# Products of a tile of weights in two groups: first with its high part, then with its low part

## The chip, the cores and the metric

The kernel runs on one core of a Trainium2 chip. The metric is device time in microseconds of one execution, the median of three runs. TensorE multiplies, VectorE, ScalarE and GpSimd work on tiles in on-chip memory, and SyncE issues the transfers from DRAM.

## The reference

Two layers of a decoder trunk on 256 tokens of 1024 features. Each layer is a feed-forward half-step, token mixing (a gated delta rule beside sparse attention, one input and one output projection), and a second feed-forward half-step; the scale, shift and gate of each come from a conditioning vector. One norm ends it. All weights are float32 and are read from DRAM once (256 MB).

```python
for l in range(DEPTH):
    mod = (cond @ ada_w[l] + ada_b[l]).reshape(B, 3, 3, D)
    h = modulate(rms_norm(x, norm_g[l, 0]), mod[:, 0, 0], mod[:, 0, 1])
    x = x + 0.5 * mod[:, 0, 2][:, None, :] * swiglu(h, ffn_w_in[l, 0], ffn_w_out[l, 0])
    h = modulate(rms_norm(x, norm_g[l, 1]), mod[:, 1, 0], mod[:, 1, 1])
    x = x + mod[:, 1, 2][:, None, :] * token_mix(h, mix_w_in[l], ..., mix_w_out[l], cos, sin)
    h = modulate(rms_norm(x, norm_g[l, 2]), mod[:, 2, 0], mod[:, 2, 1])
    x = x + 0.5 * mod[:, 2, 2][:, None, :] * swiglu(h, ffn_w_in[l, 1], ffn_w_out[l, 1])
return rms_norm(x, final_norm_g)
```

## The kernel before, in words

Products run in float32r, a shortened float32. For accuracy each operand is split in two such parts, a high one and a low one that holds what the high one lost, and a product becomes three: high with high, high with low, low with high.

**The stream of weights.** Weights come as 344 tiles of 128 partitions by up to 1024 columns (`raw`, 10 slots). `produce` (line 726) lets ScalarE make the high part (`hi`, 4 slots) and VectorE the low one (`lo<-raw,hi`, 4 slots), which waits for the high part. A tile serves 24 products on 128 x 256 columns as a rule (8 pairs of a weight block and a feature block, three products each). Between the tiles stand 36 pieces of the conditioning (`ada`): each reads 2 MB and is multiplied and summed by VectorE, and in part by ScalarE (`adb`, `raw<-raw,cond`) and GpSimd (`adb<-adb,raw`). `take` (line 753) hands the next tile to the products.

**The products.** `split_mm` (line 1018) issues three of one weight block: `hi` with the high part of the features (`hh`, `aa` or `yh`), `hi` with their low part (`hl`, the second half of `aa`, `yl`), and `lo` with the high part. `split_mm_nat` (line 1211) does it with tokens as weights, in the projections `n0` to `n2`. `early_mm` (line 1011) does it on x before its norm is known, scaled by feature: `xh` from ScalarE and `xl` from VectorE, made block by block of 128 features in `norm_xa` as the sublayer before finishes a block of x (`xT`). So a sublayer begins while the last norm is being summed (`nS`, `nsq`, `nv`, `nr`).

The feed-forward step (`ffn_body`, line 1060) has 11 units of four tiles each into two banks (gate and value side by side), then 4 units of six tiles out of the hidden features (`aa`), two banks each. `ffn_act` makes the hidden features: `sg` and `aa` on ScalarE, `av` and the low `aa` on VectorE. Token mixing (`mix_body`, line 1174) projects, runs the delta rule and the attention as streams beside each other, and `mix_out` (line 1855) projects back.

**What sets the order.** Nothing is issued where it is written. `record` (line 276) notes every instruction and what it depends on; products of one bank keep their recorded order. `schedule` (line 362) then walks a list scheduler over the whole program with estimated times, forward and backward in turn, and keeps the order whose estimated end is first. `issue` puts out that order, so every instruction has line 546 in the profile, and tiles must be told apart by name. Each engine runs its own instructions strictly in that order.

## Time and profile before

| | us |
|---|---|
| median of three runs (1206.88, 1209.07, 1210.11) | 1209.07 |
| span of the profiled execution | 1203.7 |
| TensorE busy with products | 1160.3 |
| TensorE busy with weight loads | 1080.6 |
| VectorE busy | 958.1 |
| ScalarE busy | 669.8 |
| GpSimd busy | 219.6 |

The span is of one profiled execution, from its first instruction to its last. Products and weight loads of TensorE overlap; the ends of products are modelled, so a busy TensorE may still have short gaps between the starts of products. In the names, buffer numbers are left out: `bank<-hh,lo` is a product of the features `hh` with a low part of weights into a bank.

### The profile page before, as it was taken

What the parts mean: (1) busy time and instruction counts of PE and PEld (TensorE: products, weight loads), DVE (VectorE), ACT (ScalarE), POOL (GpSimd) and SP (SyncE); (2) the same over time, 40 slices, a digit from 0 to 9 for tenths busy, and PEclk for the clock granted to TensorE, in tenths of its full rate; (3) what the DMA queues carried; (4) which work ended last, traced back from release to release, by engine and by line L of the source; (5) the groups of instructions that cost most, each with busy time, mean ns of one, the idle gap of its engine ahead of it and who ended that gap; (6) DMA issues with size and microseconds to landing.
All of it is one profiled execution on the core that took longest, in us unless ns stands there. A gap on an engine that the chain in (4) does not pass through costs nothing.

```text
span 1203.7 us, 24132 instructions
## 1 busy us (share of the span) xinstructions
PE 1160.3 (96%) x9450; PEld 1080.6 (90%) x9451; DVE 958.1 (80%) x1716; ACT 669.8 (56%) x1177; POOL 219.6 (18%) x184
## 2 busy tenths in 40 slices
PE   8998989999999999999999999999999999999997
PEld 3698989997988899999999999998797879999997
DVE  3699899898987699988978877999998669855543
ACT  2456446555585556556545454556657556644444
POOL 2033343220001233113221110233100013200001
PEclk9999999999999999999999999999999999999999
DMA  9879999985424378987976887988562235756540
GB/s 333 292 218 313 293 303 308 287 254 171 132 54 123 118 225 294 301 272 227 319 224 187 284 265 221 314 283 283 157 192 55 71 102 181 255 172 193 181 145 36
DMA packets 230758, 259.89 MB, mean 216 GB/s; under 512 B 16130, under 2 KB 190836, under 8 KB 230644
## 3 DMA queue, kind: packets, MB, share of 16 engines
q1 hardware_dynamic: 230644, 258.35, 68.0%
q8 instruction: 74, 1.21, 0.4%
q14 instruction: 40, 0.33, 0.1%
HBM read 256.09 MB, written 2.23 MB: 215 GB/s over the span
## 4 chain that ended last, share of the span: by engine, by line
PE 72%; DVE 16%; DMA 4%; issue 3%; ACT 3%; POOL 1%; DVEq 0%; POOLq 0%; ACTq 0%; SPq 0%
PE bank L546 72%; DVE lo L546 7%; DVE ada L546 2%; ACT hi L546 2%; DMA raw<-in_ffn_w_out_dram 1%; DMA raw<-in_ada_w_dram 1%; DVE qT L546 1%; DVE aa L546 1%; POOL adb L546 1%; DMA raw<-in_ffn_w_in_dram 1%; DMA w<-in_cmp_w_k_dram 1%; DVE av L546 0%; DVE hl L546 0%; DVE KL L546 0%; DVE Pt L546 0%
## 5 line engine op out<-in xcount | busy, mean ns | idle before, releaser
L546 DVE TENSOR_TENSOR lo<-raw,hi 128x1024 fp32r<-128x1024 f32 (+3 forms) x340 | 420.2, 1254 | 119.6 <-ACT hi L546 86.4
L546 ACT ACTIVATE hi<-raw 128x1024 fp32r<-128x1024 f32 (+3 forms) x340 | 344.6, 1028 | 282.1 <-PE bank L546 233.2
L546 PE MATMUL bank<-hh,lo 128*128 128x256 f32 x1440 | 380.2, 285 | 10.4 <-DVE lo L546 10.3
L546 PE MATMUL bank<-hl,hi 128*128 128x256 f32 x1440 | 385.0, 284 | 0.6 <-DVE hl L546 0.6
L546 PE MATMUL bank<-hh,hi 128*128 128x256 f32 x1440 | 384.0, 283 | 1.6 <-ACT hi L546 1.0
L546 PEld LDWEIGHTS bank<-hh,lo 128*128 128x128 f32 x1440 | 260.2, 189 | 14.4 <-DVE lo L546 13.9
L546 PEld LDWEIGHTS bank<-hh,hi 128*128 128x128 f32 x1440 | 264.1, 189 | 4.7 <-issue 1.7
L546 PEld LDWEIGHTS bank<-hl,hi 128*128 128x128 f32 x1440 | 264.2, 189 | 1.2 <-DVE hl L546 0.8
L546 PE MATMUL bank<-aa,hi 128*128 128x256 f32 x1408 | 247.7, 281 | 2.9 <-ACT hi L546 2.5
L546 PEld LDWEIGHTS bank<-aa,hi 128*128 128x128 f32 x1408 | 212.5, 189 | 3.4 <-ACT hi L546 2.7
L546 PE MATMUL bank<-aa,lo 128*128 128x256 f32 x704 | 188.4, 283 | 8.5 <-DVE lo L546 8.5
L546 POOL TENSOR_TENSOR adb<-adb,raw 128x512 f32<-128x512 f32 x65 | 98.4, 1514 | 305.2 <-ACT raw L546 283.9
L546 PEld LDWEIGHTS bank<-aa,lo 128*128 128x128 f32 x704 | 129.5, 189 | 11.2 <-DVE lo L546 11.1
L546 DVE SCALAR_TENSOR_TENSOR ada<-raw,cond,ada 128x512 f32<-128x512 f32 x131 | 111.1, 848 | 4.5 <-DMA raw<-in_ada_w_dram 3.6
L546 POOL TENSOR_TENSOR nS<-nS,nsq 128x256 f32<-128x256 f32 x42 | 42.5, 1013 | 257.8 <-ACT nS L546 184.6
L546 ACT ACTIVATE aa<-av 128x256 fp32r<-128x256 f32 x88 | 36.0, 412 | 60.7 <-DVE av L546 60.5
L546 POOL TENSOR_TENSOR ada<-ada,adb 128x512 f32<-128x512 f32 x28 | 49.7, 1773 | 104.6 <-DVE ada L546 100.6
L546 PE MATMUL bank<-xl,hi 128*128 128x258 f32 (+1 forms) x224 | 62.3, 293 | 1.3 <-DVE xl L546 1.2
L546 PE MATMUL bank<-xh,hi 128*128 128x258 f32 (+1 forms) x224 | 60.5, 289 | 2.1 <-ACT xh L546 2.1
L546 PE MATMUL bank<-xh,lo 128*128 128x258 f32 (+1 forms) x224 | 61.4, 288 | 0.0
L546 DVE TENSOR_TENSOR aa<-av,aa 128x256 fp32r<-128x256 f32 x88 | 48.5, 554 | 10.9 <-ACT aa L546 10.9
L546 PEld LDWEIGHTS bank<-xl,hi 128*128 128x128 f32 x224 | 41.6, 190 | 7.1 <-issue 4.2
(308 smaller groups left out, 1620.9 us busy)
## 6 DMA issues: line engine op xcount, KB each, us to landing
raw<-in_ffn_w_in_dram SPq DMA_DIRECT2D x172, 512.0 KB, 4.8
raw<-in_ada_w_dram SPq DMA_DIRECT2D x144, 512.0 KB, 4.9
raw<-in_ffn_w_out_dram SPq DMA_DIRECT2D x64, 512.0 KB, 4.6
raw<-in_mix_w_in_dram SPq DMA_DIRECT2D x40, 512.0 KB, 5.0
raw<-in_ffn_w_out_dram SPq DMA_DIRECT2D x32, 384.0 KB, 4.3
raw<-in_mix_w_out_dram SPq DMA_DIRECT2D x8, 512.0 KB, 4.2
raw<-in_mix_w_out_dram SPq DMA_DIRECT2D x16, 256.0 KB, 4.5
raw<-in_mix_w_in_dram SPq DMA_DIRECT2D x8, 408.0 KB, 3.8
```

What stands on the lines that cost most here:

```text
L546: r = getattr(getattr(self.tc.nc, x.engine), x.fn)(*map(bind, x.args), **{k: bind(a) for k, a in x.kw.items()})
```

## The change

`split_mm`, `split_mm_nat` and `early_mm` issued the three products of one weight block next to each other. Their successors take all the weight blocks of a tile as a list: first come all the products with `hi` (with the high and with the low part of the features), then all with `lo`. The products are the same, and so are the tiles, the slots and the transfers; the accumulation in a bank runs in another order. Comments were removed, which shifts line numbers. The rest of the file is as before.

```diff
-    def early_mm(o, wh, wl, k, n=T + 2):
...
-        PE.matmul(o[:, 0:n], wh, xh, start=k == 0, stop=False)
-        PE.matmul(o[:, 0:n], wl, xh, start=False, stop=False)
-        PE.matmul(o[:, 0:n], wh, xl, start=False, stop=k == KT - 1)
-    def split_mm(o, wh, wl, xh, xl, first, last):
...
-        PE.matmul(o, wh, xh, start=first, stop=False, skip_group_check=True)
-        PE.matmul(o, wh, xl, start=False, stop=False, skip_group_check=True)
-        PE.matmul(o, wl, xh, start=False, stop=last, skip_group_check=True)
+    def early_products(jobs, n=T + 2):
+        for o, wh, _, k in jobs:
+            PE.matmul(o[:, 0:n], wh, nst["xh"][:, k, 0:n], start=k == 0, stop=False)
+            PE.matmul(o[:, 0:n], wh, nst["xl"][:, k, 0:n], start=False, stop=False)
+        for o, _, wl, k in jobs:
+            PE.matmul(o[:, 0:n], wl, nst["xh"][:, k, 0:n], start=False, stop=k == KT - 1)
+    def split_products(jobs):
+        for o, wh, _, xh, xl, first, _ in jobs:
+            PE.matmul(o, wh, xh, start=first, stop=False, skip_group_check=True)
+            PE.matmul(o, wh, xl, start=False, stop=False, skip_group_check=True)
+        for o, _, wl, xh, _, _, last in jobs:
+            PE.matmul(o, wl, xh, start=False, stop=last, skip_group_check=True)
...
-                    for j in range(2):
-                        o, cs = qs[j][:, s * 256:(s + 1) * 256], slice(j * 128, (j + 1) * 128)
-                        for k in range(4):
-                            split_mm(o, wh[:, k, cs], wl[:, k, cs], hh[:, 4 * h + k], hl[:, 4 * h + k],
-                                     h == 0 and s == 0 and k == 0, h == 1 and k == 3)
+                    cut = [slice(j * 128, (j + 1) * 128) for j in range(2)]
+                    split_products([(qs[j][:, s * 256:(s + 1) * 256], wh[:, k, cut[j]], wl[:, k, cut[j]], hh[:, 4 * h + k],
+                                     hl[:, 4 * h + k], h == 0 and s == 0 and k == 0, h == 1 and k == 3)
+                                    for j in range(2) for k in range(4)])
...
                 for k in range(2):
                     for b in range(2):
-                        t = slice(b * 128, (b + 1) * 128)
                         kk = 2 * j + k
-                        split_mm_nat(qs[b][:, :n], hh[:, kk, t], hl[:, kk, t], wh[:, k], wl[:, k], kk == 0, kk == KT - 1)
+                        PE.matmul(qs[b][:, :n], hh[:, kk, tok[b]], wh[:, k], start=kk == 0, stop=False)
+                        PE.matmul(qs[b][:, :n], hl[:, kk, tok[b]], wh[:, k], start=False, stop=False)
+                for k in range(2):
+                    for b in range(2):
+                        kk = 2 * j + k
+                        PE.matmul(qs[b][:, :n], hh[:, kk, tok[b]], wl[:, k], start=False, stop=kk == KT - 1)
             return qs
...
```

The other places that used `split_mm` or `early_mm` (the outputs of the feed-forward step, the transposed projections, the first projection `k`, the first units, `mix_out`) are rewritten in the same way.

The list scheduler makes a new order of all engines from this. Three places of it follow; a number behind a name is that of the buffer. The first is TensorE near the end of the first feed-forward step, where the last inputs (`hh`, `hl`) and the first outputs (`aa`) mix. Before:

```order
L546 MATMUL bank_1965<-hh_451,hi_2055 128x256
L546 MATMUL bank_1965<-hl_458,hi_2055 128x256
L546 MATMUL bank_2031<-hh_451,lo_2003 128x256
L546 MATMUL bank_2108<-aa_843,hi_2090 128x256 x2
L546 MATMUL bank_2031<-hh_451,hi_1976 128x256
L546 MATMUL bank_1965<-hh_451,lo_2084 128x256
```

`lo_2084` belongs to `hi_2055` and stood six products behind its first use. The same place in the change, where `lo_2165` belongs to `hi_2139`:

```order
L546 MATMUL bank_2147<-aa_1143,hi_2139 128x256 x4
L546 MATMUL bank_2147<-aa_1280,hi_2139 128x256 x4
L546 MATMUL bank_2028<-hh_460,hi_2021 128x256
L546 MATMUL bank_2028<-hl_468,hi_2021 128x256
L546 MATMUL bank_2028<-hh_460,hi_2021 128x256
L546 MATMUL bank_2147<-aa_1143,lo_2165 128x256 x2
L546 MATMUL bank_2147<-aa_1280,lo_2165 128x256 x2
```

Eight products of the tile and three of another now stand ahead of the first one with its low part.

The second place is TensorE at the start of the last feed-forward step, the first products with x. Before:

```order
L546 MATMUL bank_12588<-xh_11113,hi_12486 128x258
L546 MATMUL bank_12588<-xh_11113,lo_12531 128x258
L546 MATMUL bank_12592<-xh_11113,hi_12518 128x258
L546 MATMUL bank_12592<-xh_11113,lo_12552 128x258
L546 MATMUL bank_12597<-xh_11113,hi_12486 128x258
L546 MATMUL bank_12588<-xl_12102,hi_12486 128x258
```

And in the change:

```order
L546 MATMUL bank_12590<-xh_11134,hi_12483 128x258
L546 MATMUL bank_12590<-xl_12130,hi_12483 128x258
L546 MATMUL bank_12590<-xh_11134,hi_12483 128x258
L546 MATMUL bank_12590<-xl_12130,hi_12483 128x258
L546 MATMUL bank_12590<-xh_11134,hi_12483 128x258
L546 MATMUL bank_12598<-xh_11134,hi_12495 128x258
```

The first product with `xl` moved from the sixth place to the second, and the low parts of the weights moved behind; each further `xh` of a bank is the next block of features.

The third place is VectorE at the same start: `xT` is x after the token mixing, `xl` its scaled low part. Before:

```order
L546 SCALAR_TENSOR_TENSOR xT<-bank,mod_6865,xT 128x256 x4
L546 TENSOR_TENSOR lo<-raw,hi 128x1024 x2
L546 SCALAR_TENSOR_TENSOR xT<-bank,mod_6865,xT 128x256 x2
L546 SCALAR_TENSOR_TENSOR xl<-xT,am,xh 128x256
L546 SCALAR_TENSOR_TENSOR xT<-bank,mod_6865,xT 128x256 x2
L546 SCALAR_TENSOR_TENSOR xl<-xT,am,xh 128x256
```

And in the change:

```order
L546 SCALAR_TENSOR_TENSOR xT<-bank,mod_6886,xT 128x256 x2
L546 TENSOR_TENSOR lo<-raw,hi 128x1024
L546 SCALAR_TENSOR_TENSOR xT<-bank,mod_6886,xT 128x256 x2
L546 TENSOR_TENSOR lo<-raw,hi 128x1024
L546 SCALAR_TENSOR_TENSOR xl<-xT,am,xh 128x256 x3
L546 SCALAR_TENSOR_TENSOR xT<-bank,mod_6886,xT 128x256 x2
```

One split of weights instead of two stands between the fourth `xT` and the first `xl`, and three `xl` come ahead of the fifth `xT`.

## Rows read from the trace of the kernel before

**Rows 1.** The page: busy us, share of the span, instructions.

```profile
span 1203.7 us, 24132 instructions
PE 1160.3 (96%) x9450; PEld 1080.6 (90%) x9451; DVE 958.1 (80%) x1716; ACT 669.8 (56%) x1177; POOL 219.6 (18%) x184
```

**Rows 2.** Windows: length; busy PE, PEld, DVE, ACT, POOL (xcount); clock; DMA share; GB/s.

```profile
60.00:90.00 30.00, 30.00 (x260) 29.85 (x259) 28.92 (x45) 16.34 (x23) 9.27 (x5) 1.00 0.71 219
1140.00:1170.00 30.00, 30.00 (x257) 30.00 (x256) 13.63 (x16) 13.14 (x16) 0.00 (x0) 1.00 0.53 169
```

**Rows 3.** Waits of weight loads, whole span: releaser, us in total, times, longest.

```profile
PEld bank L546 <- issue: 28.1, 86, 1.7
PEld bank L546 <- DVE lo L546: 25.7, 32, 2.3
...
PEld bank L546 <- ACT hi L546: 4.3, 4, 2.7
...
PEld bank L546 <- DVE xl L546: 2.7, 3, 1.4
```

**Rows 4.** Busy time by window, one for each sublayer.

```profile
51.40:250.50 199.10, 185.80 (x1539) 181.60 (x1538) 182.65 (x259) 111.49 (x168) 68.11 (x44) 0.98 0.90 290
250.50:423.60 173.10, 169.26 (x1409) 150.50 (x1402) 143.65 (x387) 111.41 (x251) 16.79 (x24) 1.00 0.46 132
423.60:623.80 200.20, 195.59 (x1633) 191.90 (x1631) 176.25 (x243) 111.53 (x170) 47.56 (x33) 1.00 0.83 269
623.80:821.90 198.10, 192.47 (x1613) 189.70 (x1611) 165.51 (x223) 104.95 (x158) 36.48 (x26) 1.00 0.82 260
821.90:1002.60 180.70, 176.28 (x1415) 152.27 (x1414) 148.35 (x384) 115.45 (x256) 23.69 (x22) 1.00 0.47 137
1002.60:1203.70 201.10, 193.16 (x1628) 191.65 (x1626) 119.50 (x171) 99.84 (x153) 17.77 (x17) 1.00 0.52 163
```

**Rows 5.** Waits of weight loads for `lo` in the four feed-forward stretches, in order.

```profile
PEld bank L546 <- DVE lo L546: 12.6, 12, 2.3
...
PEld bank L546 <- DVE lo L546: 5.1, 8, 1.1
...
PEld bank L546 <- DVE lo L546: 6.5, 9, 1.1
...
PEld bank L546 <- DVE lo L546: 1.0, 2, 0.8
```

**Rows 6.** Timeline, 168 to 178 us, of TensorE, VectorE and GpSimd: start, us.

```profile
174.88 0.50 PE L546 MATMUL bank<-aa,hi 128*128 128x256 f32 x2 [2.48 <-ACT hi L546]
175.22 0.28 PE L546 MATMUL bank<-hh,hi 128*128 128x256 f32 x1
177.09 0.58 PE L546 MATMUL bank<-hh,lo 128*128 128x256 f32 x1 [1.59 <-DVE lo L546]
...
169.61 1.51 DVE L546 TENSOR_TENSOR aa<-av,aa 128x256 fp32r<-128x256 f32 x1
...
175.82 1.21 DVE L546 TENSOR_TENSOR lo<-raw,hi 128x1024 fp32r<-128x1024 f32 x1
...
177.06 0.41 DVE L546 TENSOR_TENSOR aa<-av,aa 128x256 fp32r<-128x256 f32 x1
...
168.00 4.27 POOL L546 TENSOR_TENSOR adb<-adb,raw 128x512 f32<-128x512 f32 x3 [1.28 <-ACT raw L546]
```

**Rows 7.** Busy time by window, around that wait.

```profile
172.00:177.20 5.20, 1.12 (x8) 0.72 (x6) 5.20 (x9) 1.63 (x3) 1.66 (x2) 0.83 0.65 174
177.20:182.20 5.00, 5.00 (x24) 5.00 (x25) 4.31 (x7) 1.08 (x2) 0.00 (x0) 0.50 1.09 358
```

**Rows 8.** Start of the last feed-forward step: waits for `xl`, and VectorE's timeline.

```profile
PEld bank L546 <- DVE xl L546: 1.7, 2, 1.4
...
1002.96 0.86 DVE L546 SCALAR_TENSOR_TENSOR xT<-bank,mod,xT 128x256 f32<-128x256 f32 x2
```

More of the change, by code (lines that the diff above doesn't have):

```diff
@@ L1046, in first_unit @@
                 wh, wl = take(("fi", l, i, u), 2 * h + s)
-                for k in range(4):
-                    for j in range(2):
-                        cs = slice(j * 128, (j + 1) * 128)
-                        early_mm(qs[j][s], wh[:, k, cs], wl[:, k, cs], 4 * h + k, T if startup else T + 2)
+                cut = [slice(j * 128, (j + 1) * 128) for j in range(2)]
+                early_products([(qs[j][s], wh[:, k, cut[j]], wl[:, k, cut[j]], 4 * h + k) for k in range(4) for j in range(2)],
+                               T if startup else T + 2)
         gu = tmp([128, 2, 2, T], F32, "gu")
@@ L1203, in nat @@
                 wh, wl = take((tag, l), j)
+                tok = [slice(b * 128, (b + 1) * 128) for b in range(2)]
                 for k in range(2):
                     for b in range(2):
[L1206 removed]
                         kk = 2 * j + k
[L1208 to L1214 removed]
+                        PE.matmul(qs[b][:, :n], hh[:, kk, tok[b]], wh[:, k], start=kk == 0, stop=False)
[4 more added lines that the diff above has]
+                        PE.matmul(qs[b][:, :n], hh[:, kk, tok[b]], wl[:, k], start=False, stop=kk == KT - 1)
+            return qs
         def proj_t(tag, j):
@@ L1219, in proj_t @@
                 wh, wl = take((tag, l), 2 * j + h)
-                for c in range(2):
-                    o = q[:, c * 256:(c + 1) * 256]
-                    for k in range(4):
-                        cs = slice(c * 128, (c + 1) * 128)
-                        split_mm(o, wh[:, k, cs], wl[:, k, cs], hh[:, 4 * h + k], hl[:, 4 * h + k],
-                                 h == 0 and c == 0 and k == 0, h == 1 and k == 3)
+                cut = [slice(c * 128, (c + 1) * 128) for c in range(2)]
+                split_products([(q[:, c * 256:(c + 1) * 256], wh[:, k, cut[c]], wl[:, k, cut[c]], hh[:, 4 * h + k], hl[:, 4 * h + k],
+                                 h == 0 and c == 0 and k == 0, h == 1 and k == 3) for c in range(2) for k in range(4)])
             return q
@@ L1258, in main @@
                     wh, wl = take(("k", l), 2 * h + j)
-                    for k in range(4):
-                        for c in range(2):
-                            early_mm(qs[2 * j + c], wh[:, k, c * 128:(c + 1) * 128], wl[:, k, c * 128:(c + 1) * 128], 4 * h + k)
+                    cut = [slice(c * 128, (c + 1) * 128) for c in range(2)]
+                    early_products([(qs[2 * j + c], wh[:, k, cut[c]], wl[:, k, cut[c]], 4 * h + k) for k in range(4) for c in range(2)])
             rb = nst.pop("rbs")
@@ L1860, in mix_out @@
                 wh, wl = take(("mo", l, u), j)
-                for c in range(2):
-                    cs = slice(c * 128, (c + 1) * 128)
-                    for k in range(4):
-                        split_mm(qs[j][:, c * 256:(c + 1) * 256], wh[:, k, cs], wl[:, k, cs], yh[:, 4 * u + k], yl[:, 4 * u + k],
-                                 u == 0 and c == 0 and k == 0, u == 1 and k == 3)
+                cut = [slice(c * 128, (c + 1) * 128) for c in range(2)]
+                split_products([(qs[j][:, c * 256:(c + 1) * 256], wh[:, k, cut[c]], wl[:, k, cut[c]], yh[:, 4 * u + k], yl[:, 4 * u + k],
+                                 u == 0 and c == 0 and k == 0, u == 1 and k == 3) for c in range(2) for k in range(4)])
                 if u == 0:
```

16 lines of the change are left out of this document (4 added, 12 removed).

## The prediction

> **What bounds the kernel now.** I read the busy times first. TensorE's products are busy 1160.3 us of a span of 1203.7, VectorE 958.1 [rows 1]. A product of 256 columns costs the same whatever stands beside it: in a stretch without any wait 257 products take 30.00 us, 0.117 us each [rows 2]. The change keeps every product, so only the time between products can move, and the question is which waits stand there and where.
>
> The waits of the weight loads say which [rows 3]. One named cause stands out: the low part of a tile of weights, which VectorE makes (`lo`), 25.7 us in 32 waits. The high part, from ScalarE, costs 4.3 us in 4. Another 28.1 us in 86 short pieces are "issue", for which the profile shows no releaser; I leave them where they are.
>
> Then I cut the span into sublayers: four feed-forward stretches of about 200 us and two of token mixing [rows 4], each from its first product with x. The waits for `lo` lie in the feed-forward stretches alone: 12.6, 5.1, 6.5 and 1.0 us, 25.2 us of the 25.7 and 31 of the 32 waits [rows 5]. They go with VectorE's load there: 182.65 of 199.10 us (92%), 88%, 84% and 59% [rows 4]. VectorE can be nearly full without harm, though: from 60 to 90 us it is busy 28.92 of 30.00 us (96%) while TensorE makes 260 products without a wait [rows 2]. So in the first stretch VectorE is close to being a second bound, and in the others the waits are a matter of timing.
>
> One wait shows the timing. ScalarE's `hi` lets TensorE go on at 174.88, it makes three products, and stands until 177.09 for a `lo` that VectorE began at 175.82 [rows 6]. VectorE was late since work from its own queue stood before that `lo`, some of it stretched: an `aa` subtraction took 1.51 us at 169.61 while GpSimd added (168.00 to 172.27), and 0.41 us at 177.06 without it [rows 6].
>
> **The change, edit by edit.** *Distance from high to low.* In the order recorded before, a `lo` is wanted one or two products after its `hi`; now after all of the tile's products with `hi`, sixteen as a rule. The list scheduler has the last word. Counted over the 344 tiles in the built orders, the first `lo` product stood 9.6 products after the first `hi` product in the mean (median 8), and now stands 22.6 (median 15). The first excerpt of the order in the part on the change shows the place of the wait above. VectorE thus gets 7 products (medians) to 13 (means) more, by 0.117 us: 0.8 to 1.5 us per tile. The 31 waits have a mean of 25.2 / 31 = 0.81 us and the longest is 2.3 us [rows 5]. If nothing else moved, nearly all would be covered: a gain of up to 25.2 us. It is not all to be had, since VectorE's queue is in order and its sum of work stays, and since the scheduler spends part of the freedom: at the start of the last sublayer it now puts `xl` ahead of `lo` splits (third excerpt). The lower bound is 0, if VectorE's sum alone sets the pace. By stretch: in the first, 182.65 us of VectorE at the 96% of [rows 2] needs 190 us, so at most 9 us can go of its 12.6; in the second and third there is room for all. I take 6 + 3 + 4.5 + 0.5 = 14 us, a little over half.
>
> *Tiles held.* The `hi` slots (4) come free earlier, 61 products after the first use where it was 67; the `lo` slots are held until product 77 where it was 70, from the same count. A `lo` that comes to a slot now has 96 - 77 + 22.6 = 42 products until it is wanted, against 96 - 70 + 9.6 = 36 (four tiles of 24 products make 96): no loss.
>
> *What is late next.* When TensorE no longer waits for `lo`, the next to end last is `hi`, or the transfer behind it: the DMA engines are busy 90% of the first stretch [rows 4]. The 4.3 us of [rows 3] may stay or double; I add 2 us (0 to 4.3).
>
> *The clock.* After the wait of 172 to 177.2 us, in which TensorE was busy 1.12 of 5.20 us, its granted clock is 0.50, that is 1.2 GHz, for the next 5.00 us: 24 products, 0.208 us each [rows 7]. At 0.117 they would take 2.8 us; the dip costs 2.2 us. Half of the idle stretch is the wait for `hi` (2.48 us), which the change doesn't touch; the other part, 1.59 us, is the `lo` [rows 6]. I take 1 us (0 to 2.2). The Trainium skill, "TensorE: Matmul & The Clock Gate", section "HAM oscillation — how this bites in real kernels", has it that waits between bursts of products put the clock back to half and each next burst pays; that agrees with the row's 0.50, and by it the whole 2.2 us would come back where I count 1.
>
> *Starts of sublayers.* The first products of a sublayer use `xh` and `xl`, parts of x that ScalarE and VectorE make feature by feature. A low product of weights needs `xh` alone; it filled time while `xl` was made. Now the order asks for `xl` as the second product and for the next feature's `xh` as the third (second excerpt). At 1003 us TensorE already waits for `xl`, 1.7 us in 2 waits, since VectorE makes two `xT` before it [rows 8]. A start before had up to 12 low products in the first 25; if all are lost as filler that is 12 x 0.117 = 1.4 us, and 7 us at five starts. Against it stands the scheduler's new order on VectorE: now three `xl` follow the fourth `xT` and one `lo`, where two `lo` and two more `xT` came first. The bounds are -1.7 us (the wait goes) and +7 us; I take +1.
>
> *Token mixing.* TensorE's idle time there is 173.10 - 169.26 = 3.8 us and 180.70 - 176.28 = 4.4 us [rows 4], next to none of it for `lo`. Its chains go through other engines, and the products of weights are filler, of the same number. I take 0, and +-4 us for another order. At the very end the scheduler keeps the last but one block of features 11 products before the last, so the closing norm is untouched: 0.
>
> **The sum.** -14 - 1 + 1 + 0 + 2 = -12 us on the profiled 1203.7. The median of the runs, 1209.07, stands 5.4 us above that span; with the same 5.4 us: 1203.7 - 12 + 5.4 = 1197.1 us.
>
> **The rivals.** *The waits move on* (no change). VectorE's sum is the bound, and the scheduler gives the new distance away to other work of VectorE, as the third excerpt hints; TensorE runs ahead once in each stretch by the added 0.8 to 1.5 us and then waits again. Two stretches have VectorE near full, and what delays a `lo` there (the 1.51 us beside GpSimd's additions) is not touched. For it: 92% and 88% [rows 4]. Against: TensorE ran free at 96% [rows 2], and in the third stretch 6.5 us of waits stand at 84%. Time: -2 us, 1207. The Trainium skill, "SBUF — State Buffer", section "Who interferes with whom", has a rule on this side: a VectorE instruction with two SBUF inputs and a GpSimd instruction that reads SBUF shut each other out for the whole instruction. The trace agrees (0.41 against 1.51 us), and by this rule alone the delays would recur wherever GpSimd adds, and the time would be this rival's 1207.
>
> *The starts lose their filler* (slower). The second product waits for `xl`, the third for the next `xh`, and in-order TensorE holds all products behind them. It decides if VectorE makes the first `xl` later than TensorE's second product at most starts, as at 1003 us now. Price +7 us as above, and with the gain of the rival before (-2): 1209.1 + 5 = 1214 us. Against it: only one start waits for `xl` noticeably now.
>
> *The change doesn't do what it says*: the scheduler could have put the low products back beside the high ones. The built order excludes it (medians 8 and 15).
>
> **How the numbers follow.** A measurement of this kernel tells about 0.3% from no change, 3.6 us: faster is below 1205.4, slower above 1212.7. The forecast, 1197.1 us, gets 0.70, all of it faster; the waits that move on 0.17, the same; the lost filler 0.13, slower. The low end takes all 25.2 us with nothing coming late behind them: 1209.1 - 25 = 1184. The high end covers the second case and part of the third: 1212.
>
> **What would show it.** Waits of weight loads for `lo` fall from 25.7 us to some 11, most in the third and second stretch; waits for `hi` stay under 8; the granted clock shows no 0.50 near 175 us if the first term holds; the feed-forward stretches shorten by 3 to 6 us and the mixing ones by none; waits for `xl` stay near 2.7 us in all. Wrong would be: `lo` waits near 25 with VectorE's share up (first rival), or `xl` and `xh` waits of several us at the starts (second), or products at another pace than 0.117 us, which I exclude.

## The result

The changed kernel takes 1216.58 us, the median of four runs (1215.21 to 1220.09), beside 1207.97 us of the kernel before on the same chip. The ratio is 1.0078 with a 95% interval of 1.0057 to 1.0100: slower by 0.8%, where the forecast was 1% faster. The profiled execution has a span of 1215.5 us, 11.8 more than before; its run took 1217.27 us.

The page of the changed kernel, busy us, share and instructions (answers to [rows 1]):

```profile
span 1215.5 us, 24157 instructions
PE 1166.7 (96%) x9450; PEld 1083.0 (89%) x9451; DVE 954.9 (79%) x1716; ACT 668.8 (55%) x1177; POOL 219.7 (18%) x184
```

The engines make the same instructions as before, and VectorE, ScalarE and GpSimd are busy as long as before, within 3.2 us. TensorE is busy 6.4 us longer for the same 9450 products and idle 5.4 us longer; since the ends of products are modelled, both are time between the starts of products, and not a lower clock (0.997 in the mean, 0.995 before). The windows by sublayer, cut as before at the first product with x (answers to [rows 4]; columns: start:end, length, busy PE, PEld, DVE, ACT, POOL with instructions, granted clock, DMA share, GB/s):

```profile
46.60:247.90 201.30, 188.48 (x1550) 182.05 (x1548) 187.27 (x267) 111.55 (x169) 64.74 (x43) 0.99 0.89 289
247.90:434.00 186.10, 177.91 (x1413) 153.31 (x1407) 147.69 (x393) 114.27 (x255) 17.86 (x25) 0.99 0.44 131
434.00:634.40 200.40, 194.97 (x1618) 191.37 (x1619) 171.77 (x238) 109.39 (x165) 46.47 (x32) 1.00 0.81 264
634.40:835.20 200.80, 194.57 (x1620) 191.09 (x1619) 165.43 (x223) 105.09 (x157) 38.62 (x26) 1.00 0.80 257
835.20:1016.20 181.00, 175.74 (x1414) 151.76 (x1413) 146.22 (x391) 116.13 (x258) 26.95 (x23) 1.00 0.47 141
1016.20:1215.50 199.30, 192.01 (x1628) 191.21 (x1626) 118.66 (x166) 98.46 (x151) 16.58 (x15) 1.00 0.51 162
```

Against [rows 4]: the first mixing starts 2.6 us earlier (247.9 for 250.5) and takes 186.1 us for 173.1. The other four stretches change by +0.2, +2.7, +0.3 and -1.8 us. So the first token mixing, where the prediction took 0, lost 13 us, and the feed-forwards, where it took 14 us of gain, gained next to nothing. (Lengths in the table further on come from unrounded cuts and can differ from the windows by 0.1.)

The waits of TensorE's weight loads over the whole span (answers to [rows 3]; releaser, us in total, times, longest):

```profile
PEld bank L546 <- issue: 28.6, 94, 0.8
PEld bank L546 <- DVE lo L546: 22.4, 28, 1.8
...
PEld bank L546 <- POOL nS L546: 7.1, 5, 3.4
PEld bank L546 <- ACT hi L546: 4.9, 9, 1.6
PEld bank L546 <- ACT hh L546: 3.1, 3, 1.2
...
PEld bank L546 <- DVE xl L546: 2.3, 3, 1.3
```

The waits for low parts fell by 3.3 us only (25.7 to 22.4), and a new one stands beside them: GpSimd's sum of squares `nS`, 7.1 us, which was 0.3 before. In the four feed-forward stretches, in order (answers to [rows 5]: 12.6, 5.1, 6.5 and 1.0):

```profile
PEld bank L546 <- DVE lo L546: 9.8, 10, 1.7
...
PEld bank L546 <- DVE lo L546: 5.9, 9, 1.0
...
PEld bank L546 <- DVE lo L546: 6.3, 8, 1.8
...
PEld bank L546 <- DVE lo L546: 0.3, 1, 0.3
```

### Two places where the traces differ

VectorE's own waits in front of a low part, whole span; first the kernel before, then the changed one:

```profile
DVE lo L546 <- ACT hi L546: 86.6, 77, 5.1
DVE lo L546 <- PE bank L546: 23.1, 16, 3.2
```

```profile
DVE lo L546 <- PE bank L546: 62.0, 48, 3.2
DVE lo L546 <- ACT hi L546: 39.6, 39, 3.0
```

A wait for "PE bank" here is one for a place: one of the four buffers of low parts, which comes free with the last product that reads it. Before, VectorE mostly waited for the high part that it subtracts (86.6 us); now it mostly waits for a place (62.0 us for 23.1). In all, though, it is idle in front of low parts about as long as before, 122.2 us for 119.6: one cause took the place of another. The groups of these instructions, before and changed (count, busy us, mean ns, idle us in front and what ended it):

```profile
L546 DVE TENSOR_TENSOR lo<-raw,hi 128x1024 fp32r<-128x1024 f32 (+3 forms) x340 | 420.2, 1254 | 119.6 <-ACT hi L546 86.4 <-PE bank L546 23.1 <-ACT aa L546 3.8
```

```profile
L546 DVE TENSOR_TENSOR lo<-raw,hi 128x1024 fp32r<-128x1024 f32 (+3 forms) x340 | 425.5, 1268 | 122.2 <-PE bank L546 62.0 <-ACT hi L546 39.6 <-issue 11.9
```

The second place is the start of the first mixing. The timeline of the changed kernel (start, us, engine, operation, tiles; in brackets the idle time in front):

```profile
245.85 2.88 DVE L546 TENSOR_TENSOR lo<-raw,hi 128x1024 fp32r<-128x1024 f32 x2
...
249.53 0.47 DVE L546 SCALAR_TENSOR_TENSOR xT<-bank,gate,xT 128x256 f32<-128x256 f32 x1
...
250.52 1.21 DVE L546 TENSOR_TENSOR lo<-raw,hi 128x1024 fp32r<-128x1024 f32 x1
250.59 1.72 POOL L546 TENSOR_TENSOR nS<-nS,nsq 128x256 f32<-128x256 f32 x1 [1.26 <-ACT nsq L546]
251.65 0.47 DVE L546 SCALAR_TENSOR_TENSOR xT<-bank,gate,xT 128x256 f32<-128x256 f32 x1
...
252.37 0.79 PE L546 MATMUL bank<-ones,nS 128*128 128x128 f32 x2 [3.20 <-POOL nS L546]
```

and of the kernel before:

```profile
250.40 0.47 DVE L546 SCALAR_TENSOR_TENSOR xT<-bank,gate,xT 128x256 f32<-128x256 f32 x1
...
251.27 0.47 DVE L546 SCALAR_TENSOR_TENSOR xT<-bank,gate,xT 128x256 f32<-128x256 f32 x1
251.59 0.74 POOL L546 TENSOR_TENSOR nS<-nS,nsq 128x256 f32<-128x256 f32 x1 [0.53 <-ACT nsq L546]
...
252.51 0.38 PE L546 MATMUL bank<-ones,nS 128*128 128x128 f32 x2
```

Before, the feed-forward's last product starts at 250.1 us and the two last blocks of x (`xT`) are done at 250.9 and 251.7. Now that product starts at 247.5 us, 2.6 earlier, but VectorE has low parts between the two blocks and ends them at 250.0 and 252.1: the norm of the next sublayer is no earlier. TensorE, which is that much ahead, makes 8 first products (before: 13 stood there; at 0.117 us the five are 0.6 us) and then stands 3.20 us for `nS`. The clock falls there; windows around that wait:

```profile
247.90:252.40 4.50, 1.30 (x17) 1.07 (x11) 4.50 (x7) 2.96 (x6) 2.88 (x2) 0.94 0.97 268
252.40:255.90 3.50, 3.50 (x19) 3.50 (x20) 1.73 (x3) 0.76 (x2) 0.00 (x0) 0.59 1.05 402
```

After 4.50 us with 1.30 us of products the granted clock is 0.59 over the next 3.50 us (0.50, 1.2 GHz, but for the edges). The Trainium skill, "TensorE: Matmul & The Clock Gate", section "HAM oscillation — how this bites in real kernels", describes this: a wait between two bursts of products, and the next burst at half clock; the rows agree. The first `hh`, the normalized input that the sublayer's other products need, comes 11.7 us after the feed-forward's last product, where it was 7.0.

That start is not all of the loss. Three marks of the first mixing, the first `hh`, the delta rule's first product with `dec` and the first output product (`yh`), before and then changed:

```profile
257.11 0.51 ACT L546 ACTIVATE hh<-nt,mod 128x256 fp32r<-128x256 f32 x1 [0.62 <-DVE nt L546]
382.27 0.38 PE L546 MATMUL bank<-dec,uu 128*128 128x128 f32 x2
399.17 0.71 PE L546 MATMUL bank<-yh,hi 128*128 128x256 f32 x4
```

```profile
259.21 0.51 ACT L546 ACTIVATE hh<-nt,mod 128x256 fp32r<-128x256 f32 x1 [0.62 <-DVE nt L546]
388.09 0.38 PE L546 MATMUL bank<-dec,uu 128*128 128x128 f32 x2
407.88 0.75 PE L546 MATMUL bank<-yh,hi 128*128 128x256 f32 x4 [1.00 <-ACT yh L546]
```

The mixing starts 2.6 us earlier and its first `hh` comes 2.1 us later: 4.7 of the 13.0 us. Another 3.7 us are lost up to `dec`, 2.9 up to `yh`, and 1.7 behind it.

### The profile page after: what moved, and what is told of

It reads as the page before. It is cut to its first block, busy times and chain, and to the rows that moved or that the text cites. A ratio compares the mean times of both kernels' runs of the same rounds, so it can differ in the third digit from the quotient of the medians.

```text
span 1215.5 us, 24157 instructions
## 1 busy us (share of the span) xinstructions
PE 1166.7 (96%) x9450; PEld 1083.0 (89%) x9451; DVE 954.9 (79%) x1716; ACT 668.8 (55%) x1177; POOL 219.7 (18%) x184
## 4 chain that ended last, share of the span: by engine, by line
PE 67%; DVE 14%; DMA 5%; ACT 3%; issue 3%; POOL 1%; DVEq 0%; POOLq 0%; SPq 0%; ACTq 0%
PE bank L546 67%; DVE lo L546 6%; DMA raw<-in_ada_w_dram 4%; DVE ada L546 1%; ACT hi L546 1%; DVE kT L546 1%; POOL nS L546 1%; DVE qT L546 1%; DVE xl L546 1%; DMA raw<-in_mix_w_in_dram 0%; DVE hl L546 0%; DVE QS L546 0%; DMA raw<-in_ffn_w_in_dram 0%; DVE blk L546 0%; DVE xT L546 0%
## 5 line engine op out<-in xcount | busy, mean ns | idle before, releaser
L546 DVE TENSOR_TENSOR lo<-raw,hi 128x1024 fp32r<-128x1024 f32 (+3 forms) x340 | 425.5, 1268 | 122.2 <-PE bank L546 62.0
L546 PE MATMUL bank<-hh,hi 128*128 128x256 f32 x1440 | 348.8, 283 | 1.7 <-ACT hi L546 1.7
L546 PE MATMUL bank<-hl,hi 128*128 128x256 f32 x1440 | 347.7, 283 | 0.8 <-DVE hl L546 0.7
L546 PE MATMUL bank<-hh,lo 128*128 128x256 f32 x1440 | 248.3, 285 | 7.8 <-DVE lo L546 7.5
L546 PEld LDWEIGHTS bank<-hh,lo 128*128 128x128 f32 x1440 | 205.6, 189 | 12.3 <-DVE lo L546 10.8
L546 PE MATMUL bank<-aa,hi 128*128 128x256 f32 x1408 | 203.7, 281 | 1.1 <-ACT hi L546 1.0
L546 PEld LDWEIGHTS bank<-aa,hi 128*128 128x128 f32 x1408 | 184.4, 188 | 1.9 <-ACT hi L546 1.7
L546 PE MATMUL bank<-aa,lo 128*128 128x256 f32 x704 | 121.9, 283 | 8.2 <-DVE lo L546 8.0
L546 PEld LDWEIGHTS bank<-aa,lo 128*128 128x128 f32 x704 | 100.6, 188 | 10.7 <-DVE lo L546 10.7
L546 ACT ACTIVATE raw<-raw,cond 128x512 f32<-128x512 f32 x65 | 44.6, 712 | 8.1 <-DMA raw<-in_ada_w_dram 8.0
L546 PEld LDWEIGHTS bank<-xh,hi 128*128 128x128 f32 x224 | 41.2, 192 | 6.3 <-issue 3.4
```

The lines of the kernel that those rows point to most:

```text
L546: r = getattr(getattr(self.tc.nc, x.engine), x.fn)(*map(bind, x.args), **{k: bind(a) for k, a in x.kw.items()})
```

## The experiments

In the listings below `GROUPED` names the places where products are issued in two groups: `first` (a feed-forward's first unit), `fi` and `fo` (its bodies), `k` (the first features of a mixing), `nat`, `proj` and `mo` (the rest of a mixing). All seven are the changed kernel, none is the kernel before.

### The grouping without a new plan, and the plan without the grouping

The first run keeps before's plan and permutes TensorE's products alone; the second does the reverse to the changed kernel.

```diff
-        self.issue(self.schedule())
+        self.issue(self.regroup(self.schedule(), True, SKIP))
...
+            if grouped:
+                xs = [x for x in xs if x.mark[2] < 2] + [x for x in xs if x.mark[2] == 2]
+            else:
+                jobs = list(dict.fromkeys(x.mark[1] for x in xs))
+                xs.sort(key=lambda x: (jobs.index(x.mark[1]), x.mark[2]))
+            for n, x in zip(places, xs):
+                new[n] = x
```

> Before's recorded program and before's plan; only then, on TensorE alone, the products of one tile share the places that the plan gave them, first those with the high part, then those with the low part (308 of the 344 tiles; for the other 36 this would leave two engines waiting for each other, so they stay as they were). The first product with the low part stands 41.9 products behind the first with the high part (before: 9.6, the changed kernel: 22.6), and the low part's last product stays where it was (70 products behind the first, as before; the changed kernel: 77). Every other engine issues in before's order. Theory A (the grouping does what it should, the loss comes from the new plan that the scheduler makes for the regrouped program): 1196 to 1207 us, no longer than before, and the waits of TensorE's weight loads for a low part fall from 25.7 to under 12 us. Theory B (the grouping itself costs: its products wait for something that is ready later, or the high and low slots come free later): 1211 to 1222 us.

> The changed kernel's program and plan; only then, on TensorE alone, the products of a tile share the places of the plan job by job again, high, high, low (278 of the 344 tiles; 66 stay grouped for the same reason as above). Every other engine issues in the changed kernel's order. Low part 9.9 products behind the high part on average, median 2. Theory A (the plan is what was lost): 1214 to 1230 us, still as slow as the changed kernel or slower, since the plan stays and the waits for low parts come back (the waits of weight loads for a low part above 22.4 us). Theory B (the grouping itself costs): 1203 to 1211 us.

Measured: 1259.66 us (ratio 1.0438, 1.0404 to 1.0472) and 1392.46 us (1.1539, 1.1521 to 1.1556). Neither theory had such times. The waits of weight loads in the first:

```profile
PEld bank L548 <- ACT hi L548: 16.8, 19, 2.2
PEld bank L548 <- DVE lo L548: 12.7, 11, 2.1
...
PEld bank L548 <- ACT hh L548: 9.6, 8, 2.4
PEld bank L548 <- DVE hl L548: 7.4, 9, 2.3
PEld bank L548 <- ACT aa L548: 5.5, 2, 4.5
```

Distance does cut the waits for low parts: at 42 products they are 12.7 us, near the 11 that the prediction named. But the products with the high part have taken their places, and they want `hi`, `hh`, `hl` and `aa` sooner than engines that keep their old order deliver them: 4.3 us of waits for `hi` became 16.8, 2.6 for `hh` 9.6. In the second run the waits for low parts are 123.4 us: the changed plan has VectorE make them as late as the grouping allows. A plan and an order of products belong together, and the comparison has to be between kernels that are planned anew.

### Is it the luck of one plan?

Both kernels with another plan, by a nudge to one of the scheduler's estimates: for the plain kernel the time from VectorE to TensorE, for the grouped one the fixed part of a product (`PE_FIX`, 2.33 to 2.2 ns).

```diff
-       ("scalar", "tensor"): 275, ("vector", "tensor"): 256, ("gpsimd", "vector"): 74, ("gpsimd", "scalar"): 74,
+       ("scalar", "tensor"): 275, ("vector", "tensor"): 258, ("gpsimd", "vector"): 74, ("gpsimd", "scalar"): 74,
```

> The kernel before, with one estimate of the scheduler changed by less than one per cent (the time from VectorE's end to a TensorE that waits for it, 256 to 258 ns): the same products in the same pairs, with another plan on every engine. Low part 9.7 products behind the high part, as before (9.6). Theory A (before's plan was the best of many tried, and any new plan loses some microseconds whatever is grouped): 1211 to 1220 us. Theory B (plans are worth the same and the grouping costs): 1204 to 1210 us.

> The changed kernel, with one estimate of the scheduler changed (the fixed part of a product on TensorE, 2.33 to 2.2 ns): the same grouped products with another plan on every engine; low part 23.3 products behind the high part (the changed kernel: 22.6). Theory A (the plan, not the grouping, sets a difference of this size): a time at least 3 us away from the changed kernel's 1216.6, and lower if the new plan is the better one: 1205 to 1213 us. Theory B: 1213 to 1220 us.

Measured: plain 1205.91 us (0.9993, 0.9983 to 1.0002), grouped 1214.79 us (1.0055, 1.0035 to 1.0076). These new plans alone move either kernel by under 2 us, the grouping moves both pairs by 9. So theory A falls for these plans, and it is the grouping, with the plan that it brings. Two plans of a kernel are few, though: further on two plans of one kernel lie 15 us apart.

### A fifth place for low parts

```diff
-            lo = wp.tile([128, 1024], F32R, tag="lo", name="lo", bufs=SPB)
+            lo = wp.tile([128, 1024], F32R, tag="lo", name="lo", bufs=5)
```

> The changed kernel with five places for low parts instead of four (the high parts keep four). In the changed kernel VectorE waits 62.0 us for a place of a low part (before: 23.1), since the low part's last product now stands 77 products behind the first product of its tile (before: 70). Theory S (slots: the later release takes back the distance that the grouping gains): VectorE's waits for a place fall under 25 us, TensorE's weight loads wait under 16 us for low parts (22.4 now), and the time is 1203 to 1211 us. Theory N (starts of sublayers: without products with the low part to fill it, TensorE waits there for GpSimd's sum of squares): VectorE's waits fall as well, but the time stays at 1213 to 1219 us, with 5 to 7 us of waits for GpSimd's nS (7.1 now).

> The kernel before with five places for low parts instead of four: what the fifth place does without the grouping. Theory S: little, 1203 to 1209 us, as VectorE waits for these places 23.1 us in all there, and mostly for the high part (86.6 us). Theory N: the same; this run is the measure for the one beside it.

Measured: grouped 1199.02 us (0.9942, 0.9921 to 0.9962), plain 1209.67 us (1.0019, 1.0009 to 1.0029). With five places the grouping is worth 10.7 us in this plan, close to the 12 of the forecast, and this kernel is faster than the one before. VectorE's waits for a place fell from 62.0 to 6.2 us, TensorE's waits for low parts to 15.3 and for `nS` to 3.6. Both theories named a part that moved; the time lies 4 us below theory S's range, on its side. In front of low parts VectorE is still idle 117.3 us, now nearly all of it for high parts, so its waits for places don't measure what they cost.

It didn't hold in a second plan (the same 2.33 to 2.2):

> The grouped kernel with five places for low parts, in another plan (the scheduler's fixed part of a product 2.33 to 2.2 ns). Theory S (VectorE loses time at the places of low parts, and the first token mixing, where it is over 0.9 busy, pays for it): 1196 to 1204 us like the first such plan (1199.0), with VectorE waiting under 5 us for places of low parts in the two token mixings together. Rival P (that first plan was luck; plans scatter by some 10 us): anything from 1200 to 1216 us, above 1206 as likely as below.

Measured: 1214.08 us (1.0057, 1.0039 to 1.0076). VectorE waits 1.9 us for places in the first mixing, as theory S had it, but the time is rival P's. The first feed-forward, from the norm's first use to the mixing, in the first plan and then in the second:

```profile
45.40:243.30 197.90, 185.31 (x1551) 179.86 (x1549) 187.14 (x270) 112.63 (x170) 69.63 (x43) 1.00 0.91 297
```

```profile
50.20:253.20 203.00, 190.34 (x1537) 186.91 (x1535) 185.58 (x262) 109.83 (x168) 68.65 (x42) 0.95 0.89 285
```

The medians are 15 us apart, the two profiled spans 9.3 (1200.7 and 1210.0), and 9.9 us stand at the end of this stretch (243.3 and 253.2). Of these, 4.8 are there at its beginning (45.4 and 50.2), with the clock at 1.00 in both; the stretch itself takes 5.1 us more, with a granted clock of 1.00 in the one and 0.95 in the other. Its weight loads wait 11.2 us for low parts in the second plan, the longest 3.2 us, and 6.6 us, the longest 1.6, in the first; which wait lets the clock fall wasn't followed up. So 1199 us is what one plan gives, and no property of five places.

Places given elsewhere, or taken away:

```diff
-            hi = wp.tile([128, 1024], F32R, tag="hi", name="hi", bufs=SPB)
+            hi = wp.tile([128, 1024], F32R, tag="hi", name="hi", bufs=5)
```

> The changed kernel with five places for high parts and four for low parts: the same memory as in the run with five places for low parts, given to the other half. Theory S: 1212 to 1222 us, with VectorE still waiting 50 us or more for places of low parts. Rival P or a rival by which any fifth place helps (a longer lead of the weights): 1198 to 1208 us.

```diff
-            lo = wp.tile([128, 1024], F32R, tag="lo", name="lo", bufs=SPB)
+            lo = wp.tile([128, 1024], F32R, tag="lo", name="lo", bufs=3)
```

> The changed kernel with three places for low parts. Theory S: a clear loss, 1228 to 1255 us, VectorE waits over 100 us for places of low parts (62.0 with four, few with five), and the two token mixings take over 375 us (367.0 with four, 355.6 with five). Rival P: 1210 to 1222 us.

> The kernel before with three places for low parts. Theory S: a loss as well, but a smaller one than with the grouping, 1214 to 1235 us, since its low parts come free 7 products earlier; the difference between the grouped and the plain kernel is then larger than with four places (9 us), where with five it is -10.7 us. Rival P: 1204 to 1214 us.

Measured: a fifth place for high parts 1232.73 us (1.0208, 1.0180 to 1.0236); three places for low parts 1231.46 us grouped (1.0195, 1.0178 to 1.0213) and 1233.14 us plain (1.0209, 1.0193 to 1.0224). So not any fifth place helps: with a fifth high part VectorE waits 92.0 us for places. That it is slower than the changed kernel by 16 us was expected by nobody and stays open; its second mixing takes 194.0 us for 181.0, its last feed-forward 205.2 for 199.3. With three places both kernels lose, the grouped one as theory S had it, but the plain one loses as much, against it: the grouping is not simply the kernel that needs more places.

### First products and bodies apart

```diff
 EARLY = 1
+GROUPED = ['fi', 'fo', 'mo', 'nat', 'proj']
```

> The changed kernel, but with the products in front of each sublayer's norm (the first unit of a feed-forward, the first features of token mixing) product by product again, as before; all others grouped. Low part 21.5 products behind the high part on average. Theory N: the waits for GpSimd's nS fall from 7.1 to under 3 us, the start of the first token mixing loses no 3.4 us, and the time is 1204 to 1211 us. Theory S: 1212 to 1218 us, since nearly all tiles are still grouped and VectorE still waits some 60 us for places of low parts.

```diff
 EARLY = 1
+GROUPED = ['first', 'k']
```

> The kernel before, with only the products in front of each sublayer's norm grouped; all others product by product as before. Low part 10.7 products behind the high part on average (before: 9.6). Theory N: nearly the whole loss is here, 1211 to 1219 us, with 5 to 8 us of waits for GpSimd's nS. Theory S: 1204 to 1210 us.

Measured: all but the first products 1213.59 us (1.0061, 1.0041 to 1.0081); only the first products 1216.17 us (1.0078, 1.0062 to 1.0093). Each part alone, in the one plan that it was run in, loses most or all of it, so the losses don't add. Nor does the named wait decide: without grouped first products 5.7 us of waits for `nS` remain, and with them alone it is 1.3 us, while `hh` has 7.8 and `xl` 5.0.

### VectorE's sum of work

Where the expectations here and above speak of VectorE as 0.9 busy in token mixing or of 1053.8 us, they add up durations of its instructions, which overlap by some 100 us in all (958.1 us by busy time, [rows 1]); by busy time, where overlap counts once, VectorE is busy 83% of the first mixing (143.65 of 173.10 us in [rows 4]) and not 97%.

```diff
         V.tensor_scalar(a, r[0], cond[:, 0:1], None, op0=OP.mult)
-        for k in range(1, spread):
-            V.scalar_tensor_tensor(a, r[k], cond[:, k:k + 1], a, op0=OP.mult, op1=OP.add)
```

> The kernel before with VectorE's 131 multiply-adds of the conditioning left out (ada<-raw,cond,ada: 111.1 us of VectorE's 1053.8; of each piece only VectorE's first product and the share of ScalarE and GpSimd are computed; the output is another, the transfers and TensorE's products are the same). Theory V (VectorE sets the pace in five of six sublayers): 1130 to 1170 us. Theory L (TensorE sets the pace, and its waits for low parts come from the distance between a high part and its low part, as the prediction had it): 1190 to 1208 us, with waits for low parts still above 18 us.

> The changed kernel with the same part left out of VectorE's work. Theory V: with VectorE no longer at its limit the grouping loses no more and may gain, 3 us slower to 12 us faster than the plain kernel beside it. Theory P (what is lost is the plan's, whatever VectorE does): 4 to 14 us slower than the plain kernel beside it, as without the cut (9 us).

> The plain kernel with the same part left out, in another plan (the scheduler's fixed part of a product 2.33 to 2.2 ns): shows how far plans alone move this kernel. Theories V and P: within 6 us of the other plain one.

> The grouped kernel with the same part left out, in another plan (2.33 to 2.2 ns). Theory V: the mean of the two grouped kernels lies no more than 3 us above the mean of the two plain ones, or under it. Theory P: 4 to 14 us above it.

Measured: plain 1193.56 and 1194.10 us, grouped 1210.38 and 1208.18 us. Cutting 111 us of VectorE's work gives the plain kernel 14 us, 12 of them before the first mixing (238.3 for 250.5 us), and the grouped one about 6. Of the work left out 36.2, 33.0 and 30.7 us stood in the first three feed-forwards; in the first of the plain kernels they shorten by 12.2, -1.4 and 2.7 us. Theory V falls: VectorE's sum is a bound in the first feed-forward, and hardly elsewhere. The plain kernel has theory L's time, but not its waits for low parts (14.8 us, not over 18). The grouping loses 14 to 17 us here, more than with all of VectorE's work. The waits of weight loads in the plain and in the grouped kernel (the first of each two plans):

```profile
PEld bank L547 <- DVE lo L547: 14.8, 28, 1.2
...
PEld bank L547 <- POOL nS L547: 2.0, 2, 1.8
```

```profile
PEld bank L547 <- DVE lo L547: 15.0, 22, 3.0
...
PEld bank L547 <- POOL nS L547: 6.0, 5, 2.7
```

With an idler VectorE the plain kernel waits as little for low parts as the grouped one: little is left that the distance could cover, and what the grouping costs at the starts stays (waits for `nS`, `xh`, `xl`, `hh` and `hl`: 12.5 and 10.9 us plain, 16.6 and 14.2 grouped). These 3 to 4 us are not all of the 14 to 17; where the rest comes from isn't shown.

### Feed-forwards and token mixing apart

```diff
 EARLY = 1
+GROUPED = ['fi', 'fo']
```

> Grouped only in the bodies of the four feed-forwards; the products in front of the norms and all of token mixing product by product as before; four places for low parts. Theory M (the loss is token mixing's: there a low part keeps its place longer when grouped, and VectorE, busy over 0.9 of that stretch, waits for the place): the first token mixing takes 173 to 179 us, VectorE waits under 6 us for places there, and the four feed-forwards lose some 5 us as in the kernel that was grouped all over but in front of the norms (820.6 for 826.3 us): 1198 to 1206 us. Theory F (grouping anywhere costs, by the plan that it brings): 1209 to 1218 us.

```diff
 EARLY = 1
+GROUPED = ['mo', 'nat', 'proj']
```

> Grouped only in token mixing (its projections and its output; the first features, in front of the norm, and all of the feed-forwards product by product as before); four places for low parts. Theory M: the first token mixing takes 181 to 187 us, VectorE waits 8 to 13 us for places there, and the time is 1211 to 1218 us. Theory F: also above before, 1209 to 1218 us, but with the loss spread over the sublayers and not in the first token mixing.

Measured: feed-forward bodies only 1205.89 us (0.9984, 0.9972 to 0.9997), no difference that counts; mixing only 1211.74 us (1.0034, 1.0021 to 1.0046). The first is the most telling run of the study. Its stretch up to the first mixing and the first mixing, and the product with `nS` there:

```profile
22.10:242.80 220.70, 209.62 (x1693) 194.06 (x1693) 197.13 (x294) 118.61 (x183) 73.83 (x49) 0.98 0.92 297
242.80:429.10 186.30, 175.49 (x1408) 154.15 (x1401) 146.82 (x390) 112.38 (x253) 17.86 (x25) 0.96 0.45 130
```

```profile
248.42 0.80 PE L547 MATMUL bank<-ones,nS 128*128 128x128 f32 x2 [3.19 <-POOL nS L547]
```

The first mixing starts at 242.8 us, 7.7 earlier than before, and the other three feed-forwards shorten by 2.8, 1.9 and 0.9 us (table below): 13.3 us in all, as much as the prediction took. The first mixing then takes 186.3 us for 173.1: 13.2 us, all of it back, with not one product grouped in it. It begins with the wait of 3.19 us for `nS` and a granted clock of 0.96 over the stretch; the first `hh` stands 14.5 us behind the last product of the feed-forward (before: 7.0), at the same time of the program as before (257 us). So the 7.7 us are no gain that the mixing ever saw: TensorE is early, the first `hh` is not. Nor is lost filler the reason, since the first products are in their old order here. The other 5.5 us stand at the mixing's end: the first product with `dec` comes at 382.3 us, as before, but the first output product at 406.2 for 399.2. The window in front of it, and that product:

```profile
399.00:406.20 7.20, 6.72 (x50) 4.63 (x50) 2.81 (x7) 2.44 (x5) 1.21 (x1) 0.58 0.47 148
```

```profile
406.21 0.51 PE L547 MATMUL bank<-yh,hi 128*128 128x256 f32 x2 [0.41 <-ACT yh L547]
```

Between 389.0 and 396.1 us VectorE has six instructions of the conditioning (`ada`) among the attention's sums, where the kernel before had none; TensorE waits for the attention's `p` and `pt`, up to 1.61 us at a time, and its granted clock is 0.58 over the 7.2 us from 399.0 on. That is the order of one plan: from `dec` to `yh` the kernel before takes 16.9 us, this one 23.9, and the plain kernel replanned 21.9. In the other run the start is as before, and VectorE waits 10.5 us for places in the first mixing (before: 3.8):

```profile
DVE lo L547 <- PE bank L547: 10.5, 5, 4.8
```

So theory M is half right: token mixing is where the loss is. When only the feed-forward in front of it is grouped, 7.7 of the 13.2 us are its start and 5.5 the plan at its end, and the total lies in theory M's range for another reason than it gave. When the mixing is grouped itself, it is 6.8 us longer; that the places do this is argued and not shown, as the plain kernel replanned is 4.7 us longer with 5.3 us of waits for places.

The stretches of the kernels, cut at the first product with x, and three sums of waits, in us, each of one profiled execution. "Starts" adds the weight loads' waits for `nS`, `xh`, `xl`, `hh` and `hl`; "places" is VectorE's wait for a place of a low part in the first mixing.

| kernel | to 1st mixing | 1st mixing | 2nd ffn | 3rd ffn | 2nd mixing | last ffn | `lo` | starts | places |
|---|---|---|---|---|---|---|---|---|---|
| before | 250.5 | 173.1 | 200.2 | 198.2 | 180.6 | 201.2 | 25.7 | 10.5 | 3.8 |
| plain, replanned | 249.8 | 177.8 | 199.7 | 197.4 | 178.3 | 202.4 | 28.6 | 10.6 | 5.3 |
| changed | 247.9 | 186.0 | 200.4 | 200.8 | 181.0 | 199.3 | 22.4 | 17.1 | 8.2 |
| changed, replanned | 249.9 | 181.2 | 201.3 | 199.8 | 181.8 | 199.7 | 20.0 | 15.8 | 8.1 |
| all but first products | 250.9 | 184.2 | 197.5 | 195.8 | 181.7 | 200.2 | 19.6 | 19.8 | 12.4 |
| first products only | 244.6 | 179.3 | 201.6 | 197.4 | 184.8 | 204.9 | 22.5 | 17.7 | 5.3 |
| ffn bodies only | 242.8 | 186.3 | 197.4 | 196.2 | 180.0 | 200.3 | 21.2 | 18.6 | 5.3 |
| mixing only | 247.1 | 179.9 | 198.4 | 198.9 | 183.6 | 202.9 | 24.2 | 14.6 | 10.5 |
| grouped, 5 places | 243.3 | 176.1 | 206.2 | 196.7 | 179.5 | 198.9 | 15.3 | 12.2 | 1.5 |
| the same, replanned | 253.2 | 179.0 | 200.6 | 196.8 | 182.1 | 198.2 | 20.4 | 12.3 | 1.9 |

Read it by columns. "Starts" is 10.5 and 10.6 in the plain kernels and 14.6 to 19.8 in all six grouped ones with four places. With four places the 2nd and 3rd feed-forward are 1 to 3 us shorter where the bodies are grouped and the first products are not, and not shorter where the first products are grouped too; the kernel with no grouped feed-forward product has 198.4 and 198.9, so some 2 us are the scatter of plans. The first mixing is longest in kernels with long starts or long waits for places, and near the plain ones where a fifth place has brought both down; but the first products alone, with long starts, have 179.3 us, hardly more than the plain kernel replanned, and before's 173.1 is the shortest of all, so part of each difference to it is its plan's.

## Why the prediction was wrong

The profiled span moved by +11.8 us where -12 were forecast. Two terms miss most: the distance, taken at -14 us, and token mixing, taken at 0 with bounds of 4.

*Distance from high to low (-14 us, measured -3.3 us of waits).* This term was mis-sized. That distance covers waits is right (12.7 us are left where it is 42 products). But it was counted on the finished order as if VectorE's low parts stayed where they were. They moved back with their products: on the changed plan, with the products alone put back job by job, the waits for low parts are 123.4 us. In the stretches where 3 and 4.5 us were taken, the waits went from 5.1 to 5.9 and from 6.5 to 6.3.

*Tiles held (0).* The sum, 42 products against 36, already counts that the place comes free 7 products later (77 for 70), and no run shows it wrong. What it didn't see is that VectorE would wait for these places: 62.0 us for 23.1, and 6.2 with a fifth place. That these waits cost time is not shown: VectorE's idle time in front of low parts is 119.6, 122.2 and 117.3 us in the three kernels, whatever it waits for. A fifth place is worth 17.6 us to the grouped kernel in one plan and 0.7 in the other.

*Starts of sublayers (+1, bounds -1.7 to +7).* Measured +6.6 us of waits (10.5 to 17.1), near the upper bound, but for another reason than the text gave: not `xl` (2.7 to 2.3 us) but the norm's sum `nS` (0.3 to 7.1). The lost filler is real but small: 8 products stand in front of `nS` where 13 stood, 0.6 us of a wait of 3.20, and where the first products keep their old order the waits for `nS` are still 5.7 and 6.7 us. What the text missed is that TensorE gets to the start earlier and the norm does not: VectorE ends the last two blocks of x at 250.0 and 252.1 us, with low parts in its queue in front of each, where it ended them at 250.9 and 251.7.

*Token mixing (0, +-4).* Measured +13.0 and +0.3 us: this step failed, far outside its bounds. That TensorE is idle only some 4 us there, next to none of it for `lo`, was read as nothing to lose. But the chain through the other engines, which the text names, begins with the norm: from the first `hh` to the first product with `dec` it takes 124.6 to 128.9 us in the ten kernels of the table and the plain one with five places, so a late `hh` makes a late mixing. Of the 13.0 us, 4.7 are its start. The rest lies in the mixing: VectorE's busy time rises by 4.0 us there (143.65 to 147.69), its idle time by 9.0, and which order on which engine does it isn't shown.

*The clock (-1).* The wait at 172 us is gone, and with it its dip of 6.8 us at a granted clock of 0.50, but two dips of 3.4 us stand at 156 and 252 us, the second at the wait for `nS`: 0 for the -1. *What is late next (+2):* `hi` went from 4.3 to 4.9 us; within its bounds, and small. *The end (0):* right; from the last feed-forward's last product to the end it is 9.0 us in both kernels. *The pace:* unchanged, 257 products in 30.00 us from 1140 us on.

*The rivals.* The one that ended slower, the lost filler, gave 1214 us by +7 at the starts and -2 elsewhere; it came within 3 us of the result, but by luck: its +7 came true as 6.6 us of waits with another releaser, and the 13 us of the first mixing, most of them behind the start, weren't in it. It had 0.13. "It decides if VectorE makes the first `xl` later" was the wrong point for the waits at the starts: the norm's chain decides there. Of the first rival the part that VectorE waits elsewhere is right (for places, at 62.0 us), its bound by VectorE's sum is not: 111 us less of it give 14. The argument against the slower one, that only one start waits now, looked at the kernel before; the change itself made the starts wait, by letting TensorE arrive early.

What stays open: what makes the 8.3 us of the first mixing behind its start, the places of low parts or the order of one plan, since the plain kernel replanned loses 4.4 us there too; why the grouping loses more, and not less, when VectorE has less work; and why plans of the five-place kernel differ by 15 us. That the grouping with four places loses rests on four pairs of plans, two with all of VectorE's work and two with less.

## What to carry to other kernels

Moving a consumer later gains only as long as its producer stays where it is: a scheduler may move the producer back with it, so look at the producer's order in the new plan, and not only at the distance. A producer's waits for places tell what it waits for, not what that costs: see if its idle time in all has grown. When one engine gets to the end of a stage earlier, ask what the next stage begins with; if that is a chain over other engines which was just in time, the gain turns into a wait at its start, and in two kernels here (the changed one, and with grouped feed-forward bodies alone) the clock fell there too. Where a scheduler places the instructions, judge an edit in two or more of its plans, and do its parts one at a time.

## What was not expected of the hardware

Nothing new of the units themselves. How easily the clock falls in a kernel whose TensorE is busy 96% of the time was not expected: two dips of the changed kernel to a granted clock of 0.50 stand at single waits of 2.24 and 3.20 us, and the first feed-forward of two plans of one kernel ran at 1.00 and 0.95, the second 5.1 us longer.
